# MLP rows stored once and scaled at the up-projection, memory rows normed behind the projection, weight sums and guards re-placed

## The chip, the cores and the metric

The kernel runs on one core of a Trainium2 chip. The metric is device microseconds (us) from the first to the last instruction of one launch. TensorE (PE) multiplies, VectorE (DVE), ScalarE (ACT) and GpSimd (POOL) work on rows in SBUF, SyncE (SP) issues nearly all transfers, in program order. Every engine takes its instructions strictly in the order in which the program stands.

## The reference

One hybrid decoder layer in fp32, 1024 tokens, width 1024:

```python
h = rms_norm(x, norm_mix_g)
# mLSTM, chunks of 128: needs C, n, m of the chunk before
y_m = sigmoid(mo) * rms_norm(mlstm_chunkwise(mq, mk, mv, ig, fg))
# causal differential attention, lam from lam_q1, lam_k1, lam_q2, lam_k2
y_d = diff_attention(dq, dk, dv, lam)
# attention into 256 memory rows
mkv = rms_norm(mem, mem_g) @ w_kv
y_c = memory_cross_attention(cq, mkv)
g_m, g_d, g_c = split(sigmoid(h @ w_gate + b_gate))
x = x + (g_m*(y_m @ w_proj_m) + g_d*(y_d @ w_proj_d) + g_c*(y_c @ w_proj_c)) @ w_out
h2 = rms_norm(x, norm_mlp_g)
x = x + square(relu(h2 @ w_up)) @ w_down      # width 4096
```

## The kernel before

**Products.** Each fp32 operand is cut into a high and a low part (`split`: ACT writes the rounded high part, L124, DVE subtracts it, L126; `split2` does the same at L117 and L69), and a product is three PE passes (`mm3`, L96). The large products use seven products of sums in place of eight (`PROD`): the sums of a weight's four quarters are four POOL additions (`wino_s`, L1292 to L1295, on tiles `wraw`), those of the activations are three DVE subtractions and one on POOL (`wino_t`, L1274 to L1277, from `xr` to `xts`); the cut results are `wo` and `xo`.

**Stages**, by the profile's clock: the memory rows' keys and values and the norm of x (0 to 67 us, `phase_x` and `mem_kv`); cross attention (to 180); mLSTM (to 560), in whose stream `early` forms weight sums ahead of time; differential attention (to 1115); gates (to 1208, `wino_gates`); the three projections (to 1434, `branches`, L1667); w_out (to 1523); up (to 1850, `wino`); down (to the end, `down`).

**Order.** A scheduler writes the instructions of each engine out in one order. `pin` fixes PE's. `issue_after` and `behind` set an instruction behind another on its engine (without a wait), `held` and `evicted` do so for a split against the last eviction of PSUM. `at(p, f)` in `early` hangs a step on position p of the mLSTM's PE stream.

**Start.** `consts` loads `vecs` (all vectors of gains, transposed to the tile `vec` at L221) and `lamv`, `gbias`; then the two tiles `mx` of memory rows are loaded and normed (`norm_rows`: Square on ACT L258, a POOL power, a DVE scaling L260), then transposed (L270) and cut to `memT`.

**mLSTM.** Chunks of 128 tokens carry a state `C`; `Ch` is its cut (COPY L771, then L773 for an update, L124 and L126). `mpT` is the cut matrix of decays, from the tile `ngb`, which SP loads (L721). `early` has `pairs` (4 loads, 4 sums L1452, 7 cuts L1490, 7 stores) and `sums` (4 loads, 4 sums L1452, 4 stores), all on tiles `es`.

**Gates.** `wino_gates` evicts PSUM with DVE additions to `u` and `c` (L1247 to L1261) while `wsp` cuts weights `w`.

**MLP.** In w_out, `res` makes x (tile `gl`, L1771), stores it (`x1_d`), squares it (L1779), adds it up on POOL (`ssq`, L1780), scales it by the MLP's gains (L1782, tile `h`) and stores that too (`h2_d`). `wino` loads `h2_d` to `xr` (`load`). The row norm comes late: `rstd` multiplies `ssq` with ones on PE (`px`, 8 small products), copies the result (`st`, L1833), and uses it on the products' results. `runs` is the order of products: run 0 takes two row blocks, run 1 four. The eight PSUM banks p0 to p7 are dealt in turn, `px` takes the eighth, which is also the first bank of the next run.

## Time and profile before

| | |
|---|---|
| runs | 2155.68, 2156.96, 2160.66 us (median 2156.96) |
| the profiled execution | 2153.97 us, span 2151.7 us |
| PE, DVE, ACT, POOL busy | 98%, 72%, 49%, 29% of the span |
| mean granted clock of PE | 0.996 |

PE is busy nearly throughout, so what is read in the profile is where PE stands still or runs at a lower clock. A row of the timeline gives start, length, engine, line, operation, output and inputs, shape and count, and in brackets the idle time ahead of it with what ended it.

### The profile page before, as it was taken

To read this page: it belongs to the slowest core of one execution; us is meant where nothing else is said; L and a number is where in the kernel's file an instruction comes from. 1 tells how busy PE (TensorE), PEld (TensorE's weight loads), DVE (VectorE), ACT (ScalarE), POOL (GpSimd) and SP (SyncE) were. 2 spreads that over 40 slices of the span, in tenths; PEclk is the share of its full clock that TensorE was granted. 3 is DMA by queue.
4 is the path that set the end of the run, shared out by engine and by line. 5 is a ranking of instruction groups with operands and counts; after the bars stand their busy time and mean duration, and the time that the engine had idled before them with its cause. 6 is when DMAs were issued, how large, how long until landed. Compare 5 with 4: busy or idle time off the path is not lost.

```text
span 2151.7 us, 31481 instructions
## 1 busy us (share of the span) xinstructions
PE 2112.8 (98%) x10905; PEld 1827.4 (85%) x10905; DVE 1559.6 (72%) x2971; ACT 1057.0 (49%) x2183; POOL 615.1 (29%) x756
## 2 busy tenths in 40 slices
...
GB/s 240 48 59 169 84 119 223 246 216 180 245 135 94 90 86 85 90 96 89 94 147 113 283 309 157 267 167 215 147 123 157 201 146 159 299 173 142 156 161 108
DMA packets 183206, 340.00 MB, mean 158 GB/s; under 512 B 17633, under 2 KB 52742, under 8 KB 180998
## 3 DMA queue, kind: packets, MB, share of 16 engines
...
q14 instruction: 74, 0.61, 0.1%
...
## 4 chain that ended last, share of the span: by engine, by line
PE 75%; DVE 8%; DMA 8%; ACT 3%; issue 2%; SPq 1%; POOL 1%; DVEq 0%; ACTq 0%; POOLq 0%
PE mm L96 27%; PE p L96 26%; PE mm L1667 11%; PE sc L96 5%; PE po L96 3%; PE tp L101 2%; DMA es<-in_wq 2%; DVE w L126 1%; DVE es L1452 1%; DVE cv L678 1%; DMA xr<-h_d 1%; SPq L1462 1%; PE pr L101 1%; DMA es<-y 1%; DMA wraw<-in_wdown 1%
## 5 line engine op out<-in xcount | busy, mean ns | idle before, releaser
L96 PE MATMUL mm<-w,hT 128*128 128x384 f32 (+3 forms) x2496 | 469.3, 331 | 1.3 <-DVE dsg L129 0.7
L96 PE MATMUL mm<-hT,w 128*128 128x512 f32 x1680 | 410.5, 395 | 0.3 <-ACT gt L503 0.3
L96 PEld LDWEIGHTS mm<-w,hT 128*128 128x128 f32 x2496 | 388.8, 189 | 11.9 <-DVE dsg L129 0.9
L96 PEld LDWEIGHTS mm<-hT,w 128*128 128x128 f32 x1680 | 309.9, 189 | 61.1 <-ACT gt L503 0.7
L96 PE MATMUL p<-xo,wo 128*128 128x512 f32 x1344 | 308.7, 392 | 0.0
L96 PE MATMUL p<-xd,wo 128*128 128x512 f32 x1344 | 305.6, 389 | 0.5 <-DVE acc L69 0.5
L96 PEld LDWEIGHTS p<-xo,wo 128*128 128x128 f32 x1344 | 253.6, 189 | 53.8 <-DVE u L69 1.0
L96 PEld LDWEIGHTS p<-xd,wo 128*128 128x128 f32 x1344 | 252.0, 188 | 53.9 <-DVE acc L69 1.4
L1667 PE MATMUL mm<-xs,w 128*128 128x512 f32 x1008 | 229.0, 389 | 1.0 <-DVE u L1261 1.0
L117 ACT CAST wo<-wraw 128x896 fp32r<-128x896 f32 x124 | 117.0, 945 | 226.3 <-POOL wraw L1295 94.6
L1667 PEld LDWEIGHTS mm<-xs,w 128*128 128x128 f32 x1008 | 189.1, 188 | 40.7 <-DVE u L1261 1.5
L69 DVE TENSOR_TENSOR wo<-wraw,wo 128x896 fp32r<-128x896 f32 x124 | 148.7, 1210 | 47.0 <-ACT wo L117 47.0
L1292 POOL TENSOR_TENSOR wraw<-wraw 128x128 f32<-128x128 f32 x128 | 101.1, 790 | 214.2 <-DMA wraw<-in_wdown 101.0
L1041 ACT ACTIVATE dpe<-sc,dst,drr 128x256 f32<-128x256 f32 (+7 forms) x128 | 106.7, 834 | 97.3 <-DVE dst L1037 96.1
L126 DVE TENSOR_TENSOR w<-raw,w 128x256 fp32r<-128x256 f32 (+4 forms) x257 | 127.6, 523 | 26.8 <-ACT w L124 26.1
L124 ACT CAST w<-raw 128x256 fp32r<-128x256 f32 (+4 forms) x257 | 114.9, 488 | 40.7 <-PE mm L96 11.6
L151 POOL TENSOR_SCALAR hss<-hss 128x4 f32<-128x4 f32 x8 | 3.9, 487 | 422.0 <-ACT mscr L785 422.0
L1033 DVE CUSTOM_DVE_ANT_0 sc<-sc,tmask 128x256 f32<-128x256 f32 (+7 forms) x128 | 97.1, 759 | 13.6 <-PE sc L96 12.8
L1294 POOL TENSOR_TENSOR wraw<-wraw 128x128 f32<-128x128 f32 x128 | 96.9, 757 | 0.0
L151 POOL TENSOR_SCALAR drr<-drr 128x16 f32<-128x16 f32 x16 | 3.3, 206 | 310.5 <-DVE drr L988 290.2
L96 PE MATMUL sc<-dk,dq 128*128 128x512 f32 (+3 forms) x384 | 91.9, 347 | 0.0
L69 DVE TENSOR_TENSOR acc<-acc,p 128x512 f32<-128x512 f32 x121 | 79.9, 684 | 14.5 <-PE p L96 13.9
...
## 6 DMA issues: line engine op xcount, KB each, us to landing
...
```

The costliest lines, as they stand in the source:

```text
L69: return self.tc.keep_in_program_order(f(*a, **k))
L96: ins = self.nc.tensor.matmul(out, l, r, start=start, stop=stop)
L101: self.pin(self.nc.tensor.transpose(out, x, self.ident))
L117: self.cast = self.A.copy(hi, src).ins
L124: a = nc.scalar.copy(hi, src)
L126: return a, nc.vector.tensor_sub(lo, src, f32(hi))
L678: V.scalar_tensor_tensor(out=c, in0=x[:, q : q + 512], scalar=cw(q), in1=c, op0=ALU.mult, op1=ALU.add)
L1033: V.tensor_tensor_reduce(out=sc[:, 0:n], in0=sc[:, 0:n], in1=self.tmask[:, D - n : D], scale=1.0, scalar=-3.0e38, op0=ALU.add, op1=ALU.max ...
L1041: nc.scalar.activation(pe[c][:, 0:n], sc[:, 0:n], AF.Exp, bias=t8[:, 2 + c : 3 + c], scale=rr[:, i, c : c + 1], accum_out=t8[:, 4 + c : 5 ...
L1292: G.tensor_add(r[:, 4], r[:, 0], r[:, 3])
L1294: G.tensor_sub(r[:, 6], r[:, 1], r[:, 0])
L1667: nc.tensor.matmul(cur[u], w[:, l, c], x[:, m], start=first and i == 0, stop=last and i == 2, skip_group_check=True)
```

## The change

**Start.** `consts` runs behind the issue of the memory loads; the part for lambda is now `lambdas`, behind the first half of x. The memory rows are not scaled ahead of the transposes; their factors (`rs`) are applied where the projection leaves PSUM.

**MLP.** The scaled copy of x (L1782) and its store are gone. `load` reads `x1_d` and scales it by the gains in SBUF, half on ACT, half on DVE. The guard that set the third activation block behind the last `res` now covers DVE, ACT and POOL, and stays until both products of run 0 are issued. `px` comes two tiles later. Banks are dealt from p0.

**Sums.** The positions of `early` move. In `wino_gates` the splits stand behind the last eviction. In `branches` the banks' halves change places.

```diff
-        lv = tmp.tile([P, 256], F32, name="lamv")
+    def lambdas(self, tmp):
...
     def norm_rows(self, src, r1, scr):
-        nc.scalar.activation(scr, src, AF.Square, accum_out=r1)
+        self.scale_rows(src, r1, scr)
+        self.nc.vector.tensor_scalar_mul(src, src, r1)
...
-            nc.scalar.copy(kr, ps)
+            nc.scalar.activation(kr, ps, AF.Copy, scale=rs[t])
-            nc.scalar.activation(scr[:, 0:512], ps, AF.Square)
+            nc.scalar.activation(scr[:, 0:512], ps, AF.Square, scale=rs[t])
-                self.split(self.mv[:, t, 0, s], self.mv[:, t, 1, s], ps)
+                self.split(self.mv[:, t, 0, s], self.mv[:, t, 1, s], ps, rs[t])
...
         mem = [load(a["mem"][t * P : (t + 1) * P, :], "mx") for t in range(2)]
-        for x in mem:
-            norm(x)
-        gen = self.mem_kv(kv, tmp, mem)
+        self.consts(tmp)
+        gen = self.mem_kv(kv, tmp, mem, [norm(x, "rm", self.scale_rows) for x in mem])
         half(0)
+        self.lambdas(tmp)
...
+                with self.held():
+                    self.split(t[:, 0], t[:, 1], raws[2 * u + kk][:, 1 + self.PROD[j][0]].rearrange("p k n -> p (k n)"))
...
-        with self.tc.issue_after(self.last_stt):
-            X[2] = self.wino_x(2, load)
+        guard = ExitStack()
+        for i in self.guard.values():
+            guard.enter_context(self.tc.issue_after(i))
+        X[2] = self.wino_x(2, load)
...
-            bank = lambda j: f"p{(7 * r + j + 4) % 8}"
+            bank = lambda j: f"p{(7 * r + j) % 8}"
-                    if (r, kp, j) in ((0, 1, 2), (1, 1, 3), (1, 2, 3), (1, 3, 3)):
+                    if (r, kp, j) in ((0, 1, 4), (1, 1, 3), (1, 2, 3), (1, 3, 3)):
                         first(bank(7))
+                if n == 1:
+                    guard.close()
...
-            at(p - (16 if p > 124 else 8), load)
+            at(p - {110: 40, 124: 8}.get(p, 14), load)
-                at(p + 4 + i, lambda i=i: keep(i))
+                at(p + 3 + i, lambda i=i: keep(i))
-        for n, p in enumerate((106, 124, 202, 266, 330, 394, 458, 522)):
+        for n, p in enumerate((110, 124, 198, 262, 326, 390, 454, 518)):
-                sums(p + 10, 8, 11, *S.pop(0))
-                sums(p + (22 if n < 7 else 18), 7, 9, *S.pop(0))
+                sums(p + 8, 7, 9, *S.pop(0))
+                sums(p + 18, 7, 10, *S.pop(0))
...
-                        self.pmm.tile([P, 512], F32, tag=f"mm{g % 2 * 4 + (u + 2) % 4}", name=self.name("mm")) for u in range(4)
+                        self.pmm.tile([P, 512], F32, tag=f"mm{4 - g % 2 * 4 + u}", name=self.name("mm")) for u in range(4)
-                    self.nmm = 3
+                    self.nmm = 7
...
-                            h = op.tile([P, 512], F32, tag="h2", name=self.name("h2"))
-                            nc.scalar.activation(h, x, AF.Copy, scale=self.vec[:, R_MLP + f : R_MLP + f + 1])
-                            nc.sync.dma_start(half(self.h2d, f, hf), h)
...
-                        self.h2d[2 * kp : 2 * kp + 2].rearrange("k p n -> p k n"),
+                        self.x1d[2 * kp : 2 * kp + 2].rearrange("k p n -> p k n"),
+                    f = R_MLP + 2 * kp
+                    nc.scalar.activation(b[:, 0:2], b[:, 0:2], AF.Copy, scale=self.vec[:, f : f + 1])
+                    nc.vector.tensor_scalar_mul(b[:, 2:4], b[:, 2:4], self.vec[:, f + 1 : f + 2])
```

Three places show how the instructions move. The first is the mLSTM's first chunk on SP: `es` loads of the first pair (L1482, after L1497) against the loads of `wib` and `ngb`. Before:

```order
L695 DMA wib_347_2465<-g_dwi 128x4x128
L1482 DMA es_340_2426<-in_wq 128x256
L588 DMA g_dec_2371<-g_dd 128x32
L1482 DMA es_341_2427<-in_wq 128x256
L1482 DMA es_342_2428<-in_wq 128x256
L1482 DMA es_343_2429<-in_wq 128x256
L721 DMA ngb_349_2471<-g_dng 128x4x128
L695 DMA wib_415_2890<-g_dwi 128x4x128
L504 DMA gates<-gt_344_2452 128x512
L721 DMA ngb_422_2926<-g_dng 128x4x128
```

After, where the `es` loads stand ahead of the gate stores:

```order
L1497 DMA es_312_2236<-in_wq 128x256
L1497 DMA es_313_2237<-in_wq 128x256
L1497 DMA es_314_2238<-in_wq 128x256
L1497 DMA es_315_2239<-in_wq 128x256
L593 DMA g_dwi<-g_u_2190 32x128
L592 DMA g_dng<-g_c_2195 32x128
L594 DMA g_dd<-g_mp_2356 32x1
L703 DMA wib_347_2455<-g_dwi 128x4x128
L729 DMA ngb_349_2461<-g_dng 128x4x128
L596 DMA g_dec_2369<-g_dd 128x32
```

The `es` loads have left the place between the gate stores and the `ngb` load.

The same place on DVE, where `ks` and `mpT` are what the chunk's products read. Before:

```order
L725 TENSOR_TENSOR ngb_349_2471<-ngb_349_2471,tmaskT_101 128x512
L1452 TENSOR_TENSOR es_352_2495<-es_341_2427,es_340_2426 128x256
L129 SCALAR_TENSOR_TENSOR ks_351_2483<-tp_350_2478,g_col_2459,ks_351_2483 128x128
L1452 TENSOR_TENSOR es_340_2426<-es_340_2426,es_343_2429 128x256
L1452 TENSOR_TENSOR es_353_2496<-es_340_2426,es_341_2427 128x256
L129 SCALAR_TENSOR_TENSOR ks_351_2483<-tp_350_2478,g_col_2459,ks_351_2483 128x128
L1452 TENSOR_TENSOR es_354_2497<-es_342_2428,es_353_2496 128x256
L129 SCALAR_TENSOR_TENSOR ks_351_2483<-tp_350_2478,g_col_2459,ks_351_2483 128x128 x2
L744 TENSOR_TENSOR ngb_349_2471<-ngb_349_2471,tp_355_2502 128x512
L1490 TENSOR_TENSOR es_340_2426<-es_340_2426 128x256
L126 TENSOR_TENSOR mpT_356_2516<-ngb_349_2471,mpT_356_2516 128x512
```

After:

```order
L733 TENSOR_TENSOR ngb_349_2461<-ngb_349_2461,tmaskT_58 128x512
L129 SCALAR_TENSOR_TENSOR qp_348_2458<-wib_347_2455,qp_348_2458 128x512
L606 COPY g_col_2449<-tp_345_2445 128x96
L129 SCALAR_TENSOR_TENSOR ks_351_2473<-tp_350_2468,g_col_2449,ks_351_2473 128x128 x4
L752 TENSOR_TENSOR ngb_349_2461<-ngb_349_2461,tp_352_2485 128x512
L126 TENSOR_TENSOR mpT_353_2499<-ngb_349_2461,mpT_353_2499 128x512
L1467 TENSOR_TENSOR es_354_2514<-es_313_2237,es_312_2236 128x256
L1467 TENSOR_TENSOR es_312_2236<-es_312_2236,es_315_2239 128x256
```

The sums now stand behind the cut of `mpT`.

The second place is the start of the MLP on DVE: `gl` is the last w_out tile, `xts` and `xo` the third block's sums and cuts, `wo` cut weights, `st2` the copy of `px`, `dg` its use. Before:

```order
L1771 SCALAR_TENSOR_TENSOR gl_2857_16499<-mm_2856_16474,gl_2857_16499 128x512
L1274 TENSOR_TENSOR xts_2872_16679<-xr_2871_16677 128x512
L126 TENSOR_TENSOR xo_2873_16684<-xr_2871_16677,xo_2873_16684 128x3x512
L1276 TENSOR_TENSOR xts_2872_16679<-xr_2871_16677,xts_2872_16679 128x512
L1277 TENSOR_TENSOR xts_2872_16679<-xr_2871_16677,xts_2872_16679 128x512
L1833 COPY st2_16759<-px_2886_16750 128x8
L69 TENSOR_TENSOR wo_2887_16788<-wraw_2876_16698,wo_2887_16788 128x7x128
L126 TENSOR_TENSOR xo_2873_16684<-xts_2872_16679,xo_2873_16684 128x4x512
L1838 TENSOR_SCALAR dg_16858<-ident_68,st2_16759 128x128
```

After:

```order
L1786 SCALAR_TENSOR_TENSOR gl_2842_16444<-mm_2841_16419,gl_2842_16444 128x512
L1823 TENSOR_SCALAR xr_2855_16623<-xr_2855_16623,vec_119 128x1024
L1285 TENSOR_TENSOR xts_2856_16627<-xr_2855_16623 128x512
L1287 TENSOR_TENSOR xts_2856_16627<-xr_2855_16623,xts_2856_16627 128x512
L126 TENSOR_TENSOR wo_2859_16643<-wraw_2851_16603,wo_2859_16643 128x7x128
L1288 TENSOR_TENSOR xts_2856_16627<-xr_2855_16623,xts_2856_16627 128x512
L126 TENSOR_TENSOR xo_2857_16632<-xr_2855_16623,xo_2857_16632 128x3x512
L69 TENSOR_TENSOR wo_2868_16680<-wraw_2858_16637,wo_2868_16680 128x7x128
L126 TENSOR_TENSOR xo_2857_16632<-xts_2856_16627,xo_2857_16632 128x4x512
L1848 COPY st2_16713<-px_2870_16704 128x8
L69 TENSOR_TENSOR wo_2871_16736<-wraw_2860_16646,wo_2871_16736 128x7x128
L1853 TENSOR_SCALAR dg_16808<-ident_105,st2_16713 128x128 x3
```

The copy `st2` stood ahead of the 128x4x512 cut of the third block and now stands behind it.

The same place on POOL: `ssq` is the sum of squares, `wraw` are weights, `xts` is the third block. Before:

```order
L1275 TENSOR_TENSOR xts_2872_16679<-xr_2871_16677 128x512
L1780 TENSOR_TENSOR ssq_13576<-ssq_13576,sq_2850_16433 128x512
L1780 TENSOR_TENSOR ssq_13576<-ssq_13576,sq_2854_16468 128x512
L1292 TENSOR_TENSOR wraw_2888_16791<-wraw_2888_16791 128x128
L1294 TENSOR_TENSOR wraw_2888_16791<-wraw_2888_16791 128x128
L1293 TENSOR_TENSOR wraw_2888_16791<-wraw_2888_16791 128x128
L1295 TENSOR_TENSOR wraw_2888_16791<-wraw_2888_16791 128x128
L1780 TENSOR_TENSOR ssq_13576<-ssq_13576,sq_2858_16503 128x512
L1292 TENSOR_TENSOR wraw_2876_16698<-wraw_2876_16698 128x128
L1294 TENSOR_TENSOR wraw_2876_16698<-wraw_2876_16698 128x128
L1293 TENSOR_TENSOR wraw_2876_16698<-wraw_2876_16698 128x128
L1295 TENSOR_TENSOR wraw_2876_16698<-wraw_2876_16698 128x128
```

After:

```order
L1795 TENSOR_TENSOR ssq_13566<-ssq_13566,sq_2843_16448 128x512
L1303 TENSOR_TENSOR wraw_2858_16637<-wraw_2858_16637 128x128
L1305 TENSOR_TENSOR wraw_2858_16637<-wraw_2858_16637 128x128
L1304 TENSOR_TENSOR wraw_2858_16637<-wraw_2858_16637 128x128
L1306 TENSOR_TENSOR wraw_2858_16637<-wraw_2858_16637 128x128
L1303 TENSOR_TENSOR wraw_2860_16646<-wraw_2860_16646 128x128
L1286 TENSOR_TENSOR xts_2856_16627<-xr_2855_16623 128x512
L1304 TENSOR_TENSOR wraw_2860_16646<-wraw_2860_16646 128x128
L1305 TENSOR_TENSOR wraw_2860_16646<-wraw_2860_16646 128x128
L1306 TENSOR_TENSOR wraw_2860_16646<-wraw_2860_16646 128x128
```

The last sum of squares now stands ahead of the weight sums and of the third block's `xts`, which stood far ahead of it.

The same place on ACT, from the last square of w_out on; `pt` (L1382) and `u2` are evictions of PSUM, L117 and L124 the casts of weights and blocks. Before:

```order
L1779 ACTIVATE sq_2858_16503<-gl_2857_16499 128x512
L1782 ACTIVATE h2_2859_16506<-gl_2857_16499,vec_79 128x512
L117 CAST wo_2887_16788<-wraw_2876_16698 128x7x128
L124 CAST xo_2873_16684<-xts_2872_16679 128x4x512
L1382 COPY pt0_16775<-p0_2877_16704 128x512
L1382 COPY pt1_16776<-p1_2878_16705 128x512
```

After:

```order
L1794 ACTIVATE sq_2843_16448<-gl_2842_16444 128x512
L1822 ACTIVATE xr_2855_16623<-xr_2855_16623,vec_119 128x1024
L124 CAST wo_2859_16643<-wraw_2851_16603 128x7x128
L124 CAST xo_2857_16632<-xr_2855_16623 128x3x512
L117 CAST wo_2868_16680<-wraw_2858_16637 128x7x128
L117 CAST wo_2871_16736<-wraw_2860_16646 128x7x128
L124 CAST xo_2857_16632<-xts_2856_16627 128x4x512
L1397 COPY pt0_16723<-p0_2861_16652 128x512
```

Between the last square and the cast of the block's last four sums stood one weight cast and the old scaling; now the new scaling, the block's first cast and three weight casts stand there.

The third place is a later chunk of the mLSTM on DVE, at the first copy of the state `C`; `es` are the 512-wide sums of `sums`. Before:

```order
L1452 TENSOR_TENSOR es_504_3399<-es_504_3399,es_503_3398 128x512
L725 TENSOR_TENSOR ngb_589_3910<-ngb_589_3910,tmaskT_101 128x512
L771 COPY C_521_3506<-sc_520_3499 128x258
L126 TENSOR_TENSOR Ch_522_3508<-C_521_3506,Ch_522_3508 128x258
L781 TENSOR_TENSOR den_523_3511<-den_523_3511,g_col_2459 128x1
L782 RECIPROCAL den_523_3511<-den_523_3511 128x1
L1452 TENSOR_TENSOR es_525_3530<-es_514_3480,es_513_3479 128x512
L773 SCALAR_TENSOR_TENSOR C_527_3545<-C_521_3506,g_dec_2371,sc_526_3535 128x258
L1452 TENSOR_TENSOR es_513_3479<-es_513_3479,es_516_3482 128x512
L126 TENSOR_TENSOR Ch_528_3547<-C_527_3545,Ch_528_3547 128x258
```

After:

```order
L1467 TENSOR_TENSOR es_501_3353<-es_501_3353,es_500_3352 128x512
L1467 TENSOR_TENSOR es_516_3472<-es_510_3426,es_509_3425 128x512
L779 COPY C_522_3505<-sc_521_3498 128x258
L1467 TENSOR_TENSOR es_509_3425<-es_509_3425,es_512_3428 128x512
L126 TENSOR_TENSOR Ch_523_3507<-C_522_3505,Ch_523_3507 128x258
L1467 TENSOR_TENSOR es_510_3426<-es_509_3425,es_510_3426 128x512
```

The second group of `es` sums moves from behind the first `Ch` to both sides of the copy `C`.

59 lines of the change are left out of this document (30 added, 29 removed).

## The prediction

> **What bounds the kernel now.** I read the busy times first, then the chain of work that ended last, then what PE waited for, then the stretches and single instructions around those waits.
>
> ```profile
> PE 2112.8 (98%) x10905; PEld 1827.4 (85%) x10905; DVE 1559.6 (72%) x2971; ACT 1057.0 (49%) x2183; POOL 615.1 (29%) x756
> PE 75%; DVE 8%; DMA 8%; ACT 3%; issue 2%; SPq 1%; POOL 1%; DVEq 0%; ACTq 0%; POOLq 0%
> ```
>
> PE is busy for 98% of the span and carries 75% of the chain (the next, DVE and DMA, 8% each). The change leaves the products themselves alone, so it can only win time in which PE stands still or runs below full clock. The first is a list of waits.
>
> ```profile
> PE tp L270 <- DVE mx L260: 5.0, 2, 4.9
> PE px L96 <- POOL ssq L1780: 4.9, 1, 4.9
> PE sc L96 <- ACT mpT L124: 3.1, 1, 3.1
> PE sc L96 <- DVE Ch L126: 2.2, 4, 1.2
> PE mm L96 <- DVE u L1252: 1.5, 1, 1.5
> PE sc L96 <- ACT Ch L124: 1.4, 3, 0.7
> PE mm L1667 <- DVE u L1261: 1.0, 1, 1.0
> PE mm L96 <- DVE c L1247: 0.6, 2, 0.4
> ```
>
> The columns are total us, times, longest. Nearly every wait that the edits aim at stands here once, with its price. The second is the clock, the column after POOL's in the table of stretches:
>
> ```profile
> 256.00:268.00 12.00, 8.91 (x33) 7.13 (x32) 7.59 (x21) 6.28 (x19) 0.00 (x0) 0.72 0.51 177
> 1523.00:1546.00 23.00, 17.82 (x72) 14.60 (x71) 11.09 (x10) 13.09 (x17) 17.80 (x22) 0.78 0.53 176
> 1546.00:1850.00 304.00, 303.98 (x1348) 251.20 (x1347) 255.57 (x304) 144.41 (x210) 197.19 (x261) 1.00 0.48 166
> ```
>
> Two waits, of 3.1 and 4.9 us, are followed by a granted clock of 0.72 and 0.78 in their stretch, so they cost more than they last. In the up-projection behind them PE is busy 303.98 of 304 us: 1348 products in that time are 0.226 us each, the price of a wide product below.
>
> **The change part by part.** All sums are against the profiled execution's 2153.97 us (2.27 us of it outside the span of 2151.7). It lies 2.99 us under the median of 2156.96, which I add at the end.
>
> *Start: 2.2 us saved, ends 0 and 4.9.*
>
> ```profile
> 0.72 0.39 SPq L242 DMA_DIRECT2D lamv<-in_lamv  x1
> 2.08 1.36 SPq L320 DMA_DIRECT2D mx<-in_mem  x2
> 7.88 1.06 ACT L258 ACTIVATE scr<-mx 128x1024 f32<-128x1024 f32 x1 [3.19 <-DMA mx<-in_mem]
> 10.40 1.04 ACT L124 CAST w<-raw 128x1024 fp32r<-128x1024 f32 x1
> 13.12 2.36 DVE L126 TENSOR_TENSOR w<-raw,w 128x1024 fp32r<-128x1024 f32 x2
> 12.05 0.69 PE L270 MATMUL tp<-ident,mx 128*128 128x128 f32 x2 [4.87 <-DVE mx L260]
> 14.38 1.22 PE L96 MATMUL mm<-w,memT 128*128 128x512 f32 x2
> ```
>
> The memory loads are issued at 0.72 in place of 2.08, and the Square and the first weight's cast follow the load: 10.40 becomes 9.04, ending at 10.1. The scalings that hold PE until 12.05 go, and PE's 4.87 us wait with them. But DVE's order now has the first weight's subtraction (1.2 us, half of 2.36) ahead of the copy to `vec`, which every cut of `memT` needs: subtraction to 11.3, copy and cut to 12.2, where 0.9 is an estimate below the 1.6 us between the end of the first transposes (12.74) and the first product, in which the cut lay. The first product then starts at 12.2 instead of 14.38. The row factors are applied in instructions that run anyway. Lambda's six small instructions go behind the first half of x, where the splits ahead of them are what PE has in store; if that cover is gone they cost a wait as long as they are, small against the 4.9. If the weight loads decide, nothing is won; if `vec` did not matter, PE's whole 4.87.
>
> *First chunk of the mLSTM: 5.9 us saved, ends 2 and 6.5.*
>
> ```profile
> 247.16 2.61 SPq L1482 DMA_DIRECT2D es<-in_wq  x3
> 249.87 0.38 SPq L721 DMA_DIRECT2D ngb<-g_dng  x1
> 254.50 0.69 DVE L725 TENSOR_TENSOR ngb<-ngb,tmaskT 128x512 f32<-128x512 f32 x1 [5.33 <-DMA ngb<-g_dng]
> 260.07 1.31 PE L96 MATMUL sc<-va,mpT 128*128 128x258 f32 x3 [3.09 <-ACT mpT L124]
> 261.18 5.32 PE L96 MATMUL mm<-hT,w 128*128 128x512 f32 x12
> 266.30 0.61 PE L96 MATMUL sc<-va,ks 128*128 128x258 f32 x3
> ```
>
> The `ngb` load waited behind three `es` issues for 2.6 us, its consumer stood idle until 254.50, and then four `es` sums and a cut stood between it and `mpT`. Afterwards neither is there: the load comes 2.6 us earlier and five DVE instructions are out of the way, against a wait of 3.09. The wait goes, and with it the slow clock behind it: 12 products took 5.32 where 12 x 0.226 are 2.71, 2.6 lost, and the three `sc` took 1.31 against 0.61, 0.7 lost. 3.09 + 2.6 + 0.7 = 6.4 (the upper end, rounded up). What is late next is the first `Ch`, as in other chunks (rows above, longest 1.2); I leave 0.5 for it. The lower end is a wait that stays at 1 with most of the clock loss.
>
> *Other sums of the mLSTM: 1.5 us saved, ends -4 and 3.6.*
>
> ```profile
> 517.64 0.69 DVE L1452 TENSOR_TENSOR es<-es,es 128x512 f32<-128x512 f32 x1 [4.09 <-DMA es<-y]
> 519.23 0.39 PE L96 MATMUL sc<-Ch,qp 128*128 128x258 f32 x1 [0.68 <-ACT Ch L124]
> 520.78 0.50 PE L96 MATMUL sc<-Ch,qp 128*128 128x258 f32 x2 [1.17 <-DVE Ch L126]
> ```
>
> DVE waits up to 4.09 us for an `es` load, and the update of `C` that PE needs stands behind that. Of that PE waited 0.68 + 1.17 = 1.85. The sum of all `Ch` waits in the list is 3.6 us. The second group of sums is moved to both sides of the first copy of `C`, away from the later updates, but the load's lead stays at 7 positions for the second group and falls from 8 to 7 for the first (a position is three products, 0.68 us). So a wait can as well come back at the first copy. I take two fifths of the waits, since more leaves the updates than comes to the copy; the lower end is six first groups later by 0.68 us, 4.1, of which most reaches PE.
>
> *Gates: 1.8 us saved, ends 0 and 2.1.*
>
> ```profile
> 1115.00:1208.00 93.00, 90.01 (x393) 72.61 (x391) 57.57 (x101) 46.47 (x97) 25.56 (x32) 1.00 0.48 156
> 1137.15 4.15 DVE L126 TENSOR_TENSOR w<-fr,w 128x256 fp32r<-128x256 f32 x5 [1.44 <-ACT w L124]
> ```
>
> Five splits ran ahead of the eviction that PE waited for at L1252. With `held` a split issued behind an eviction stays behind it; the sum of the two waits is 2.1, of which one small `c` wait may stay. The cover for the splits is DVE's idle time (57.57 of 93 us busy); if it is gone, weights come late and nothing is won.
>
> *Banks in the projections: 1.0 us saved, ends 0 and 1.0.* The first projection tiles no longer take the banks that the gates' last evictions hold, so the L1261 wait of 1.0 goes. Elsewhere the rotation is the same.
>
> *Start of the MLP: 2.1 us saved, ends -1.3 and 6.9.*
>
> ```profile
> 1531.51 1.14 POOL L1292 TENSOR_TENSOR wraw<-wraw 128x128 f32<-128x128 f32 x1 [3.99 <-DMA wraw<-in_wup]
> 1534.46 0.46 POOL L1295 TENSOR_TENSOR wraw<-wraw 128x128 f32<-128x128 f32 x1
> 1534.87 1.26 POOL L1780 TENSOR_TENSOR ssq<-ssq,sq 128x512 f32<-128x512 f32 x1
> 1523.73 1.29 POOL L1275 TENSOR_TENSOR xts<-xr 128x512 f32<-128x512 f32 x1 [7.96 <-DMA xr<-h_d]
> 1536.18 1.87 PE L96 MATMUL px<-ones,ssq 128*128 128x1 f32 x8 [4.94 <-POOL ssq L1780]
> 1537.91 6.31 PE L96 MATMUL p<-xo,wo 128*128 128x512 f32 x16
> 1537.93 0.94 ACT L117 CAST wo<-wraw 128x896 fp32r<-128x896 f32 x1 [6.52 <-POOL wraw L1295]
> 1538.78 1.89 ACT L124 CAST xo<-xts 128x2048 fp32r<-128x2048 f32 x1
> 1540.71 2.29 DVE L126 TENSOR_TENSOR xo<-xts,xo 128x2048 fp32r<-128x2048 f32 x1 [0.61 <-ACT xo L124]
> ```
>
> Before, the stretch lost 23 - 17.82 = 5.2 us idle, 16 products took 6.31 against 3.62 (2.7), and `px`, by the same ratio, 0.8 of its 1.87: 8.7. The 16 scalings and 16 stores go, and ACT no longer waits for a free `h` buffer ahead of the casts and squares. The up-products begin at 1523.0; eviction and square of the last tile I estimate at 0.8 us each from instructions of that width (0.69 at 254.50), `ssq` with its 1.26 ends at 1525.9. `px` is two tiles later, at 1523.0 + 36 x 0.226 = 1531.2, so it waits for nothing, and PE comes to the next run's first tile 1.8 us of `px` and 6 products later, at 1534.35. That tile has `px`'s bank, so it needs the copy `st2`, and this stands on DVE behind the third block's last cut. Queued in that chain, by the rows: POOL's four weight sums, which took from 1531.51 to 1534.92, to 1529.4; one of the next four at 0.46 and `xts` at 1.29 to 1531.1; the other three at 0.46 to 1532.5; ACT's weight cast 0.94 and block cast 1.89 to 1535.3; DVE's cut 2.29 to 1537.6. PE waits 3.3 us, a little longer than the 3.09 that brought half clock, and pays 3.3 for that as at the first chunk: 6.6 against 8.7. With all of POOL's additions at 0.46 the copy comes at 1536.1, a wait of 1.8 with the clock kept: 6.9 saved. With both sets slow it comes at 1539.2, and with 0.61 more at each of three hand-overs, as at 1540.71, at 1541: 6.7 + 3.3 = 10.0, a loss of 1.3. I take one slow set and one fast because the rows have both and DVE is full with the block's scaling and cuts only at first. The new scaling (1.06 on ACT, like the Square of that size at 7.88; DVE's half no row gives, at most 1.2 as a subtraction of that size) lies within this chain for the third block; for the first two it lies under w_out's products, and if that cover is gone the up-projection starts later by as much.
>
> The trace has 3.09 us of idle time followed by half clock. The Trainium skill, "TensorE: Matmul & The Clock Gate", Part 1, section "The HAM clock gate", says that the clock falls after at least one idle window of about 3.4 us, and that the windows run free of the kernel. By that rule a new wait of 3.3 us would leave the clock alone, and the sum would be 3.3 larger; the 3.09 us row speaks against it, and the sum here goes by the row.
>
> Sum: 2.2 + 5.9 + 1.5 + 1.8 + 1.0 + 2.1 = 14.5, so 2139.5 us against the profiled execution, and with 2.99 for the median 2142.5.
>
> **The rivals.**
> 1. *The copy comes early enough.* POOL's short additions, a wait of 1.8 and no slow clock: 4.8 more saved, 2137.7. For it: the row of 0.46; against it: the row of 1.14, while DVE works.
> 2. *The copy's wait leaves the clock alone.* Then only 3.3 is paid: 3.3 more saved, 2139.2. For it: the forecast wait is hardly longer than the shortest that brought half clock; against it: both long waits in this trace did bring it. The Trainium skill's rule (page and section as above) is this rival's reason beside the rows.
> 3. *One new wait at a first copy of `C`.* A stop of 3.09 with its slow clock costs 6.4, and the 1.5 is not won: 2150.4. For it: DVE waited 4.09 on a load; against it: only 1.85 us of that reached PE.
> 4. *Slower than before.* Load leads of 7 positions (4.8 us) are too short for the first groups: the 4.09 us wait reached PE for 1.85, so 2.24 are covered, and a wait of DVE of 2.24 + 3.09 = 5.3 us stops PE long enough for half clock. At three of the twelve groups that is 19.2, with the 1.5: 2163.2; from three on it decides.
> 5. *The start and the banks don't do what they say:* the weight loads, not the norm, set the first product, and another eviction holds the projections: 2142.5 + 2.2 + 1.0 = 2145.7.
>
> **How the numbers follow.** The forecast has 0.40, rivals 1 to 5 have 0.20, 0.10, 0.17, 0.06 and 0.07. The range 2130 to 2154 holds all but rival 4 and the tails of 1 and 3: below 2137.7 it reaches by the other upper ends (start 2.7, sums 2.1, and most of the rest), above 2150.4 by the lower end of the first chunk (3.9). A measurement of this kernel tells about 0.2% (4.3 us) from no change: faster means under 2152.6. The forecast, 1, 2 and 5 are faster, and of rival 3, whose centre lies 2.2 below that, some six tenths: faster 0.87, same 0.07, slower 0.06.
>
> **What would show it.** The first product starts near 12.2 us. No wait of a `sc` for `mpT`, and a clock of 1.00 from 256 to 268. No L1252 and L1261 waits on PE. `px` without a wait, and in its place a wait of a `p` tile for the `st` copy, of 2 to 6 us, with a clock under 0.9 behind it. Wrong would be: a clock below 1.00 anywhere in the mLSTM, a `memT` wait as long as before, or a `p` that waits for weights in the up-projection.

## The result, and the profile after

| | before | after |
|---|---|---|
| median of the runs | 2156.96 us | 2145.61 us |
| lowest, highest (5 runs each) | 2155.68, 2162.48 | 2142.31, 2150.22 |
| the profiled execution | 2153.97, span 2151.7 | 2145.61, span 2143.8 |

The ratio of the times is 0.9944 [0.9923, 0.9964]: 11.35 us less by the medians, 8.36 by the two profiled executions. The forecast was 2142.5 in 2130 to 2154. The page's busy times and chain, and the list of waits of PE, of the changed kernel:

```profile
PE 2110.5 (98%) x10905; PEld 1827.3 (85%) x10905; DVE 1561.0 (73%) x2973; ACT 1050.6 (49%) x2171; POOL 618.9 (29%) x756
PE 82%; DVE 7%; DMA 5%; ACT 3%; issue 2%; POOL 1%; SPq 1%; DVEq 0%; ACTq 0%; POOLq 0%
PE p L96 <- ACT pt L1397: 6.0, 1, 6.0
PE sc L96 <- ACT Ch L124: 4.1, 2, 3.4
PE tp L277 <- DVE vec L224: 2.4, 1, 2.4
PE mm L96 <- DVE va L126: 1.3, 3, 0.6
```

PE now carries 82% of the chain instead of 75%. Four of the waits shown of before are gone from the list: `px` for `ssq` (4.9), `sc` for `mpT` (3.1), `mm` for `u` at the gates (1.5) and at the projections (1.0). The one for `mx` (5.0) is halved, now for `vec`; but PE's wait for the load of the vectors ahead of it, in neither extract, grew from 6.7 to 8.0. Two are new or much longer: a product tile `p` of the up-projection waits 6.0 us, a `sc` waits 3.4 for `Ch`. `va` grew from 0.3 to 1.3. The stretches around the first chunk, the last chunks and the start of the MLP (columns as in the prediction; the clock stands after POOL):

```profile
252.00:268.00 16.00, 16.00 (x88) 13.83 (x86) 11.29 (x33) 8.78 (x27) 0.00 (x0) 1.00 0.60 197
520.00:560.00 40.00, 36.18 (x211) 31.63 (x209) 25.20 (x64) 17.62 (x49) 2.08 (x2) 0.96 0.58 186
1515.00:1546.00 31.00, 24.98 (x111) 20.51 (x110) 20.93 (x25) 15.58 (x19) 23.82 (x29) 0.89 0.27 86
```

The first chunk runs at full clock without a gap (16.00 of 16 us busy); the last chunks and the MLP's start do not (0.96 and 0.89).

A view of one operand gives the first and the last start of the products that read it. The same products run in both kernels, so their starts split the span. Before, then after:

```profile
L96 PE MATMUL sc<-mkT,cqT x96: 277/283/387, 74.3 to 139.9; 128*128 128x256 f32 x96
L96 PE MATMUL sc<-va,mpT x96: 278/283/583, 260.1 to 565.0; 128*128 128x258 f32 x96
L1667 PE MATMUL mm<-xs,w x1008: 387/389/504, 1205.9 to 1435.5; 128*128 128x512 f32 x168
L96 PE MATMUL sc<-mkT,cqT x96: 277/283/385, 73.1 to 138.5; 128*128 128x256 f32 x96
L96 PE MATMUL sc<-va,mpT x96: 278/282/288, 255.5 to 562.8; 128*128 128x258 f32 x96
L1682 PE MATMUL mm<-xs,w x1008: 389/389/389, 1200.7 to 1429.0; 128*128 128x512 f32 x168
```

Worked out in this way for every kernel of this study: A up to the first `mkT` product, B from there to the first `mpT`, C from the first to the last `mpT` (the mLSTM's chunks), D to the first `xs` (differential attention and gates), E over the `xs` products (projections), F from the last `xs` to the end of the span (w_out and the MLP).

| us | A | B | C | D | E | F |
|---|---|---|---|---|---|---|
| before | 74.3 | 185.8 | 304.9 | 640.9 | 229.6 | 716.2 |
| after | 73.1 | 182.4 | 307.3 | 637.9 | 228.3 | 714.8 |
| e1 copy first | 72.5 | 182.5 | 306.2 | 637.6 | 228.3 | 715.5 |
| e2 evictions first | 72.2 | 182.8 | 308.5 | 637.5 | 228.2 | 714.9 |
| e3 old sums | 73.4 | 184.8 | 305.3 | 638.3 | 228.2 | 715.9 |
| e4 first pair only | 72.3 | 182.5 | 302.7 | 637.7 | 228.2 | 715.3 |
| e5 stores later | 73.1 | 182.5 | 299.9 | 639.4 | 228.3 | 716.8 |
| e6 gates undone | 72.9 | 182.4 | 307.3 | 642.3 | 229.5 | 714.9 |
| e7 vec first | 73.5 | 183.3 | 303.7 | 640.5 | 228.2 | 716.0 |
| e8 evictions, first pair | 73.4 | 182.5 | 304.5 | 639.1 | 228.2 | 715.7 |
| e9 start undone | 74.3 | 182.3 | 303.3 | 640.3 | 228.3 | 717.0 |
| e10 MLP undone | 73.3 | 182.3 | 305.4 | 639.6 | 228.2 | 711.3 |
| e11 all remedies | 72.4 | 182.0 | 303.9 | 637.9 | 228.2 | 710.4 |

Each is one execution. Kernels that share a stage's code show what that is worth: E agrees within 0.1 us, C of the changed table of sums (after, e1, e2, e6, e7, e9, e10) runs from 303.3 to 308.5, D of the changed gates from 637.5 to 640.5, F of the changed MLP (after, e3 to e7, e9, where F isn't touched) from 714.8 to 717.0. A difference of 2 or 3 us in C, D or F from one trace alone says little.

By the table, the 7.9 us between the two spans are 1.2 in A, 3.4 in B, -2.4 in C, 3.0 in D, 1.3 in E and 1.4 in F. C before held the slow clock behind the `mpT` wait (3.3 by the prediction's rows); that gain is in C too, so the rest of C lost 5.7 in this pair of traces.

**The last chunk**, where most of that is. Timeline of SP, DVE and PE of the changed kernel (`y` is the loaded operand of `sums`, `xc_d` their store):

```profile
543.47 2.25 SPq L1485 DMA_DIRECT2D xc_d<-es  x3
545.82 0.95 SPq L1477 DMA_DIRECT2D es<-y  x2
550.04 0.69 DVE L1467 TENSOR_TENSOR es<-es,es 128x512 f32<-128x512 f32 x1 [4.66 <-DMA es<-y]
552.52 0.48 DVE L781 SCALAR_TENSOR_TENSOR C<-C,g_dec,sc 128x258 f32<-128x258 f32 x1
553.49 1.01 PE L96 MATMUL sc<-Ch,qp 128*128 128x258 f32 x3 [3.40 <-ACT Ch L124]
554.34 4.51 PE L96 MATMUL mm<-hT,w 128*128 128x512 f32 x12
```

The last two loads stand on SP behind three stores of the group before (2.25 us, from 543.47 on; the last of the four sums to be stored runs on DVE only at 544.69). DVE idles 4.66 us on them, and behind the sums stands the update of `C` (L781), for whose cut PE waits 3.40 us. Behind it 12 products take 4.51 where 2.71 is full clock (1.8 lost). The `sc` take 1.01 against 0.52 in the chunk before, which is no slow clock: in e5 and e9 below they take 0.97 and 1.00 at the same place with the clock at 1.00. Together 3.40 + 1.8 + 0.5 = 5.7.

**The start of the MLP.** Timelines of PE, DVE, ACT and POOL of the changed kernel:

```profile
1516.55 8.32 PE L96 MATMUL p<-xo,wo 128*128 128x512 f32 x36
1524.71 1.84 PE L96 MATMUL px<-ones,ssq 128*128 128x1 f32 x16
1534.08 14.14 PE L96 MATMUL p<-xo,wo 128*128 128x512 f32 x54 [6.02 <-ACT pt L1397]
1531.61 2.29 DVE L126 TENSOR_TENSOR xo<-xts,xo 128x2048 fp32r<-128x2048 f32 x1 [5.26 <-ACT xo L124]
1533.82 0.16 DVE L1848 COPY st<-px 128x8 f32<-128x8 f32 x1
1529.61 1.89 ACT L124 CAST xo<-xts 128x2048 fp32r<-128x2048 f32 x1
1531.41 3.50 ACT L1397 COPY pt<-p 128x512 f32<-128x512 f32 x7
1518.30 1.30 POOL L1795 TENSOR_TENSOR ssq<-ssq,sq 128x512 f32<-128x512 f32 x1 [4.15 <-ACT sq L1794]
1522.68 0.79 POOL L1306 TENSOR_TENSOR wraw<-wraw 128x128 f32<-128x128 f32 x1
1523.43 1.97 POOL L1303 TENSOR_TENSOR wraw<-wraw 128x128 f32<-128x128 f32 x1
1525.36 2.13 POOL L1286 TENSOR_TENSOR xts<-xr 128x512 f32<-128x512 f32 x1
1527.45 0.46 POOL L1304 TENSOR_TENSOR wraw<-wraw 128x128 f32<-128x128 f32 x1
1531.82 2.39 POOL L1306 TENSOR_TENSOR wraw<-wraw 128x128 f32<-128x128 f32 x1
```

`px` runs without a wait. Six products later PE stops for 6.02 us, and 54 products then take 14.14 us where 54 x 0.226 are 12.2: 1.9 of slow clock, 7.9 together. The bracket names the eviction `pt`, whose seven copies ran from 1531.41 on; the copy `st` at 1533.82 to 1533.98 ends just ahead of PE's start. Which of the two PE needed is what the first experiment asks.

### The profile page after: what moved, and what is told of

Read it like the earlier page. It is cut to its first block, busy times and chain, and to the rows that moved or that the text cites. A ratio compares the mean times of both kernels' runs of the same rounds, so it can differ in the third digit from the quotient of the medians.

```text
span 2143.8 us, 31457 instructions
## 1 busy us (share of the span) xinstructions
PE 2110.5 (98%) x10905; PEld 1827.3 (85%) x10905; DVE 1561.0 (73%) x2973; ACT 1050.6 (49%) x2171; POOL 618.9 (29%) x756
## 3 DMA queue, kind: packets, MB, share of 16 engines
HBM read 214.15 MB, written 94.40 MB: 144 GB/s over the span
## 4 chain that ended last, share of the span: by engine, by line
PE 82%; DVE 7%; DMA 5%; ACT 3%; issue 2%; POOL 1%; SPq 1%; DVEq 0%; ACTq 0%; POOLq 0%
PE mm L96 34%; PE p L96 26%; PE mm L1682 11%; PE sc L96 5%; PE po L96 3%; PE tp L101 2%; DMA es<-in_wq 1%; DVE w L126 1%; DMA raw<-in_wkv 1%; DVE cv L686 1%; DMA es<-y 1%; DVE es L1467 1%; DMA ngb<-g_dng 1%; PE pr L101 1%; DVE acc L69 1%
## 5 line engine op out<-in xcount | busy, mean ns | idle before, releaser
L117 ACT CAST wo<-wraw 128x896 fp32r<-128x896 f32 x124 | 116.9, 945 | 226.7 <-PE p L96 92.7
L1303 POOL TENSOR_TENSOR wraw<-wraw 128x128 f32<-128x128 f32 x128 | 100.8, 788 | 205.6 <-DMA wraw<-in_wdown 99.9
L124 ACT CAST w<-raw 128x256 fp32r<-128x256 f32 (+4 forms) x257 | 116.4, 488 | 45.1 <-PE mm L96 11.8
L1041 DVE CUSTOM_DVE_ANT_0 sc<-sc,tmask 128x256 f32<-128x256 f32 (+7 forms) x128 | 97.1, 758 | 13.1 <-PE sc L96 12.2
L1305 POOL TENSOR_TENSOR wraw<-wraw 128x128 f32<-128x128 f32 x128 | 94.6, 739 | 0.0
L1306 POOL TENSOR_TENSOR wraw<-wraw 128x128 f32<-128x128 f32 x128 | 88.8, 694 | 10.0
```

The source lines that it names most:

```text
L117: self.cast = self.A.copy(hi, src).ins
L124: a = nc.scalar.copy(hi, src)
L1041: V.tensor_tensor_reduce(out=sc[:, 0:n], in0=sc[:, 0:n], in1=self.tmask[:, D - n : D], scale=1.0, scalar=-3.0e38, op0=ALU.add, op1=ALU.max ...
L1303: G.tensor_add(r[:, 4], r[:, 0], r[:, 3])
L1305: G.tensor_sub(r[:, 6], r[:, 1], r[:, 0])
L1306: G.tensor_sub(r[:, 7], r[:, 2], r[:, 5])
```

## The experiments

Ratios are against the kernel before on the same chip.

**e1: the copy ahead of the third block's last cut.** The split of `xts` is set behind the copy `st`.

```diff
-        self.split(xo[:, 3:7, 0], xo[:, 3:7, 1], t)
+        late.append(lambda: self.split(xo[:, 3:7, 0], xo[:, 3:7, 1], t))
...
+                    if (r, kp, j) == (0, 1, 4):
+                        with self.tc.issue_after(self.stc):
+                            rest[0]()
```

> The changed kernel with one instruction order altered: on VectorE the copy of the row norm's product (st) stands ahead of the third block's last cut; ScalarE's order stays. Theory: the 6.0 us wait of PE at the start of the up-projection, which the list of waits puts down to ScalarE's evictions pt, ends with the copy st, since its next product starts at 1534.08 and the copy ends at 1533.98. Then PE takes its first tile of the second run at once and waits one tile later for the first pt, which ends at 1531.9: a wait of about 3 us, and 2 us less in all. Rival (the list is right, pt ends it): the wait stays at 6.0 and the first tile of the second run starts at 1534.

One run: 2144.41 us (before on this chip 2155.54). Timeline of DVE and PE:

```profile
1524.49 0.17 DVE L1855 COPY st<-px 128x8 f32<-128x8 f32 x1 [0.23 <-PE px L96]
1529.98 14.58 PE L96 MATMUL p<-xo,wo 128*128 128x512 f32 x51 [3.32 <-ACT pt L1404]
```

The copy came right behind `px`, at 1524.49 instead of 1533.82, and PE's wait fell from 6.02 to 3.32: the copy was what PE waited for, and the evictions are next in line. But 51 products then took 14.58 us against 11.5 at full clock: 3.1 of slow clock where 1.9 stood behind the longer wait. Wait and clock together are 6.4 against 7.9, and F is 715.5 against 714.8: nothing that a trace can tell.

**e2: the evictions ahead too.** As e1, and ACT's cast stands behind the first run's evictions. The edit also sets the fourth block and the `dg` scalings behind the third block's last cut on DVE.

```diff
-                    A.copy(t, m)
-                wsp(n)
+                    c = A.copy(t, m)
+                with self.tc.issue_after(self.stc), self.tc.issue_after(c.ins):
+                    self.cut = rest[0]()[1].ins
+                    wsp(n)
```

> The changed kernel with the third block's last cut (ScalarE and VectorE) and the fifth weight's set behind both the copy st and the seven evictions pt. Theory: the wait of 6.0 us and the 1.7 us of slower products behind it go, none takes their place, so 7 to 8 us less than the changed kernel: near 2138, ratio to before 0.991. Rival (the block's cut, started later, is late for the fifth product group): the wait only moves 9 us on, less than 3 us saved, near 2144.

2144.35 us (2140.10 to 2145.92), ratio 0.994 [0.9927, 0.9953]. Timeline of PE:

```profile
1526.62 13.91 PE L96 MATMUL p<-xo,wo 128*128 128x512 f32 x60
1543.97 0.91 PE L96 MATMUL px<-dg,ones 128*128 128x128 f32 x4 [3.00 <-DVE dg L1861]
```

The stop is gone: 60 products run through in 13.91 us. The next is 17 us on: the `dg` tiles made from `st`, which the edit set back on DVE, stop PE for 3.00. The wait has moved, as the rival said (near 2144), and F stays at 714.9.

**e3: the old table of sums in the changed kernel.**

```diff
-            at(p - {110: 40, 124: 8}.get(p, 14), load)
+            at(p - (16 if p > 124 else 8), load)
...
-        for n, p in enumerate((110, 124, 198, 262, 326, 390, 454, 518)):
+        for n, p in enumerate((106, 124, 202, 266, 330, 394, 458, 522)):
...
-                sums(p + 8, 7, 9, *S.pop(0))
-                sums(p + 18, 7, 10, *S.pop(0))
+                sums(p + 10, 8, 11, *S.pop(0))
+                sums(p + (22 if n < 7 else 18), 7, 9, *S.pop(0))
```

> The changed kernel with the old table of positions for the weight sums in the mLSTM; all else as changed. Theory: the table wins 6.5 at the first chunk and gives back 5.5 in the later chunks, above all with one wait of 3.4 us and slow clock at the last chunk: so within 2 us of the changed kernel, 2145 to 2148, with the first chunk's 3.1 us wait for mpT back and no wait over 1.5 us in the later chunks. Rival (the last chunk's wait is chance of one execution): 6 us slower than the changed kernel, 2152.

2148.29 us (2146.05 to 2152.30), ratio 0.9967 [0.9957, 0.9977]. The list of waits of PE:

```profile
PE sc L96 <- ACT mpT L124: 2.3, 1, 2.3
```

The `mpT` wait is back (B is 2.4 longer), the one of 3.4 in the last chunk is not there. The whole table is worth about 2 us by the trace (span 2145.9 against 2143.8), 2.7 by the medians and some 5 by the ratios, whose intervals overlap (0.9957 to 0.9977 and 0.9923 to 0.9964). By the traces it is small because the table wins at the first chunk and loses at the last.

**e4: the new place for the first pair only**, the old table for the rest:

```diff
-            at(p - {110: 40, 124: 8}.get(p, 14), load)
+            at(p - {110: 40, 124: 8}.get(p, 16), load)
...
-        for n, p in enumerate((110, 124, 198, 262, 326, 390, 454, 518)):
+        for n, p in enumerate((110, 124, 202, 266, 330, 394, 458, 522)):
```

(and `sums` as in e3.)

> The changed kernel with the old table but for the first pair of sums, which stands at position 110 and loads 40 positions ahead as in the change. Theory: the first chunk's wait stays away and the later chunks are as before, so about 5.5 us less than the changed kernel: near 2140, ratio 0.992. Rival (the later chunks' waits come with the new first pair or are chance): no difference from the changed kernel, 2145.

2143.61 us (2140.53 to 2145.72), ratio 0.9938 [0.9925, 0.9951]. B is as short as in the changed kernel (182.5) and C 302.7, less than in any kernel with the changed table; e8 and e11, which have the same table, show 304.5 and 303.9. By the means the later groups' new positions cost some 2 us of C (306.0 over the seven with the changed table, 303.7 over these three), but single kernels of the two groups overlap, and the timed ratio shows what the rival said, no difference (0.9938 against 0.9944).

**e5: one number of the table.** The stores of the first group of `sums` in each round go three positions later, from p + 17 to p + 20, and so behind the second group's loads at p + 18.

```diff
-                sums(p + 8, 7, 9, *S.pop(0))
+                sums(p + 8, 7, 12, *S.pop(0))
```

> The changed kernel with one number altered: in the mLSTM the stores of each first group of weight sums stand 3 positions later, so that on SP the loads of the second group go ahead of them. Theory: the 3.4 us wait for Ch at the last chunk comes from these stores, which wait on SP for late sums and hold back the second group's loads (es<-y, 4.7 us late on VectorE). With the loads first, VectorE no longer waits over 2 us there, PE's wait falls under 1 us, and with the slow clock behind it some 4 to 5 us go: near 2141. Rival (the loads are late because the first group's own loads are): the wait stays over 2.5 us and the time at 2145.

2142.81 us (2141.67 to 2146.50), ratio 0.9947 [0.9933, 0.9961]. Timeline of DVE and PE in the last chunk:

```profile
542.87 2.15 DVE L1467 TENSOR_TENSOR es<-es,es 128x512 f32<-128x512 f32 x3 [1.85 <-DMA es<-y]
547.85 0.97 PE L96 MATMUL sc<-Ch,qp 128*128 128x258 f32 x3 [2.24 <-ACT Ch L124]
548.66 2.91 PE L96 MATMUL mm<-hT,w 128*128 128x512 f32 x12
```

DVE's wait falls from 4.66 to 1.85, PE's from 3.40 to 2.24, and no slow clock follows (12 products in 2.91 against 4.51). C is 299.9, 3.4 below the shortest with the changed table.

The six other kernels with that table (e1, e2, e6, e7, e9, e10) have the same order on SP. There DVE waits 3.86 to 4.49 us at this place and PE 2.29 to 2.90, with half clock behind it in four and none in e7 (2.50) and e9 (2.29); in the kernels with the old later table (before, e3, e4, e8, e11) PE doesn't stop here; there it waits a chunk earlier, 0.68 to 1.55 and then 1.17 or 1.18 us. So the stores ahead of the loads are shown as the cause of DVE's wait. Of PE's stop they are a part only: the theory wanted it under 1 us, and 2.24 are left, since DVE works without a break from 542.87 to the update of `C` at 546.88, on four sums and four weights' cuts that stand ahead of it. In the timed runs e5 can't be told from the changed kernel.

**e6: gates and banks undone.**

```diff
-                with self.held():
-                    self.split(t[:, 0], t[:, 1], raws[...])
+                self.split(t[:, 0], t[:, 1], raws[...])
...
-    tag=f"mm{4 - g % 2 * 4 + u}"
+    tag=f"mm{g % 2 * 4 + (u + 2) % 4}"
...
-                    self.nmm = 7
+                    self.nmm = 3
```

> The changed kernel without the hold on the gates' weight splits and with the old banks in the projections; all else as changed. Theory: the waits for u at L1252 (1.5 us, now another line number) and L1247, and the 1.0 us wait of the first projection tile come back: 3 to 4 us more than the changed kernel, near 2149, and the gates and the head of the projections show 4.2 us more lost time. Rival (these waits were chance of the order that the scheduler writes, not of hold and banks): less than 1 us of them comes back, 2146.

2150.92 us (2148.23 to 2153.92), ratio 0.9983 [0.9974, 0.9992]. The list of waits of PE:

```profile
PE mm L96 <- DVE c L1236: 1.5, 1, 1.5
PE mm L96 <- DVE u L1236: 1.5, 1, 1.5
```

The gates' waits are back, D is 642.3 and E 229.5. This is the only part whose undoing the timed runs show: the intervals of the ratios do not touch (0.9964 and 0.9974), and their middles are 0.39% (8 us) apart, the medians themselves 5.3. By the traces it is 3.6 in D (against the mean, 638.7, of the kernels with the changed gates) and 1.3 in E, 4.9 together, where the prediction put it at 2.8. What makes the rest of the 8 us no trace shows. Hold and banks were undone together; by its place, the 1.3 in E is the banks'.

**e7: the copy to `vec` ahead of the first weight's cut.**

```diff
+        with self.tc.issue_after(self.vc):
+            w = self.load_w(a["wkv"][0], 512, 2)
```

> The changed kernel with the copy to vec ahead of the first weight's subtraction on VectorE. Theory: the first product of the memory projection starts 1 to 2 us earlier (12.46 becomes 10.5 to 11.5), but the transposes of the first keys (28.5) stay within 0.4 us, since the later weights' loads set them: the start's gain is limited by these loads, not by vec. Rival (vec is what eats the forecast gain): the keys' transposes come 1 us or more earlier, and the whole start with them.

One run: 2147.04 us (before on this chip 2154.73). Timelines of PE, changed kernel first, then e7:

```profile
12.46 3.83 PE L96 MATMUL mm<-w,memT 128*128 128x512 f32 x10
28.50 0.43 PE L310 MATMUL tp<-ident,kr 128*128 128x128 f32 x2 [1.24 <-DVE kr L307]
12.25 4.28 PE L96 MATMUL mm<-w,memT 128*128 128x512 f32 x10 [2.10 <-ACT memT L128]
25.74 0.63 PE L311 MATMUL tp<-ident,kr 128*128 128x128 f32 x3 [1.21 <-DVE kr L308]
```

The first product gains 0.2 only, since `memT` is then late: on ACT its cut stands behind the second weight's cast. The keys' transposes come 2.8 us earlier, and at the first `mkT` product nothing of it is left (A is 73.5 against 73.1). Neither theory had this. What takes the lead back between the two was not followed.

**e8: e2 and e4 together,** with one more guard on POOL and the eight `dg` scalings moved from DVE to ACT.

```diff
+                if n == 1:
+                    with self.tc.issue_after(self.pw_):
+                        raw()
...
-                    wsp(n)
+                    wsp(n, more=n > 0)
```

(`pw_` is POOL's power of the row norm, so that it runs ahead of the next weight sums.)

> Both remedies together: the old table of sums but for the first pair, and at the start of the up-projection the copy st and the evictions ahead of the third block's last cut, with the eight scalings dg on ScalarE and the row norm's power ahead of one more set of weight sums on POOL. Theory: the mLSTM as in the run with the first pair only (5 us less lost than in the changed kernel), the 6.0 us wait gone, and the 3.0 us wait for dg that took its place in the run with the evictions first gone too: 10 to 12 us less than the changed kernel, 2133 to 2136, ratio 0.990. Rival (VectorE and POOL are full in the first 25 us of the up-projection, so some wait of 2 to 3 us comes back at the third or fourth block): 5 to 7 us less, 2139 to 2141.

2141.33 us (2139.99 to 2145.20), ratio 0.9936 [0.9922, 0.9949]. The `dg` stop is gone, and the next comes (timeline of PE):

```profile
1546.43 4.63 PE L96 MATMUL p<-xo,wo 128*128 128x512 f32 x10 [3.12 <-DVE wo L69]
```

3.12 us for a weight's cut, 10 products then in 4.63 instead of 2.26. The wait has moved a second time, and the time is near the rival's (2139 to 2141), not the theory's.

**e9: the start undone** (`consts` ahead of the memory rows, the rows scaled ahead of the transposes).

```diff
-            nc.scalar.activation(kr, ps, AF.Copy, scale=rs[t])
+            nc.scalar.copy(kr, ps)
...
-        gen = self.mem_kv(kv, tmp, mem, [norm(x, "rm", self.scale_rows) for x in mem])
+        for x in mem:
+            norm(x)
+        gen = self.mem_kv(kv, tmp, mem)
```

> The changed kernel with the start as before (vectors, lambda and gate bias loaded first, memory rows normed ahead of their transposes); all else as changed. Theory: the 1.9 us that the first product gained are mostly given back by 73 us, where the changed kernel was 1.2 us ahead, so about 1.2 us more than the changed kernel: 2146 to 2147, which a measurement can hardly tell from no difference. Rival (the start is worth what its first wait was, 4.9 us): 2150.

2146.61 us (2142.72 to 2147.35), ratio 0.9966 [0.9954, 0.9977]. A is 74.3 as before, against 72.2 to 73.5 in the others (mean 72.9): by that mean the start is worth 1.4 us, too little for the timed runs, whose intervals overlap.

The others fall into two groups. In e1, e2, e4 and e11 A is 72.2 to 72.5; in the changed kernel, e3, e5, e6, e8 and e10 it is 72.9 to 73.4. The stretch from 34 to 42 us tells them apart, here in e4 and in the changed kernel:

```profile
34.00:42.00 8.00, 6.18 (x31) 4.45 (x32) 5.92 (x14) 5.87 (x12) 4.70 (x9) 1.00 0.40 159
34.00:42.00 8.00, 6.77 (x28) 5.33 (x29) 5.23 (x13) 5.32 (x10) 4.75 (x9) 0.79 0.45 180
```

The granted clock is 1.00 in the first group and 0.79 in the second. So the start is worth 1.8 to 2.1 us where the clock stays up and 0.9 to 1.4 where it falls; the kernel before and e9 kept it up (1.00). Only e7, with its other order, has 73.5 at full clock.

**e10: the MLP undone**: the scaled copy stored, the old guard, `px` and banks, in the changed kernel.

```diff
+                            h = op.tile([P, 512], F32, tag="h2", name=self.name("h2"))
+                            nc.scalar.activation(h, x, AF.Copy, scale=self.vec[:, R_MLP + f : R_MLP + f + 1])
+                            nc.sync.dma_start(half(self.h2d, f, hf), h)
...
-            bank = lambda j: f"p{(7 * r + j) % 8}"
+            bank = lambda j: f"p{(7 * r + j + 4) % 8}"
...
-                    if (r, kp, j) in ((0, 1, 4), (1, 1, 3), (1, 2, 3), (1, 3, 3)):
+                    if (r, kp, j) in ((0, 1, 2), (1, 1, 3), (1, 2, 3), (1, 3, 3)):
```

> The changed kernel with w_out and the start of the up-projection as before (scaled copy of x stored and loaded, guard on VectorE alone, px two tiles earlier, old banks); all else as changed. Theory: the old 4.9 us wait of px with its slow clock comes back and the 6.0 us wait for the copy st goes, so the loss there is 8 to 9 us in place of 8: within 1.5 us of the changed kernel, 2145 to 2147. Rival (the 16 stores less also make the stages around it faster, or the slow clock costs more before): 4 us or more above the changed kernel.

2142.54 us (2139.62 to 2147.70), ratio 0.9956 [0.9943, 0.9968]. Neither theory held: the wait of 4.9 at `px` does not come back, and F is 711.3, the shortest but one. A row of PE in e10, ACT's last scaling but one in the kernel before and in e10, what followed it before on DVE and SP, and the transfers of the scaled copy around that place (size, median us to landing), before and e10:

```profile
1525.37 1.05 PE L96 MATMUL px<-ones,ssq 128*128 128x1 f32 x8 [0.24 <-POOL ssq L1791]
1524.99 0.72 ACT L1782 ACTIVATE h<-gl,vec 128x512 f32<-128x512 f32 x1 [5.74 <-DMA h_d<-h]
1514.18 0.72 ACT L1793 ACTIVATE h<-gl,vec 128x512 f32<-128x512 f32 x1 [1.74 <-DMA h_d<-h]
1526.58 1.89 DVE L126 TENSOR_TENSOR wo<-wraw,wo 128x896 fp32r<-128x896 f32 x1 [8.06 <-ACT wo L124]
1528.50 1.36 SPq L1306 DMA_DIRECT2D wraw<-in_wup  x3
h_d<-h SPq DMA_DIRECT2D x5, 256.0 KB, 7.4
h_d<-h SPq DMA_DIRECT2D x6, 256.0 KB, 3.8
```

The order on POOL around `ssq` is the same in both programs. In the kernel before, ACT's scaling waited 5.74 us for a buffer whose store was slow (7.4 us, median of five); behind it on ACT stood a weight's cast, behind that on DVE its cut (to 1528.47), behind that on SP the next weights' loads (1528.50), and behind these on POOL the four weight sums from 1531.51 on, with `ssq` last (1534.87, in the prediction's rows). The last square was not what `ssq` waited for: it ended at 1530.80. In e10 the stores landed in 3.8, ACT waited 1.74, and `px` 0.24. By these rows the 8.7 us that the prediction read at this place were largely the price of a late store, not of the old order alone. Why the stores land sooner in e10 was not tried, and one trace each does not tell whether they do so in every execution.

**e11: all remedies**: e2 and e4, the `dg` tiles made on ACT, and the fourth block's and a weight's cuts set behind the work that PE waits for.

```diff
-                        for t in range(NT):
-                            V.tensor_scalar_mul(dg[:, t], self.ident, st[:, t : t + 1])
+                    with self.tc.issue_after(self.xsc):
+                        for t in range(NT):
+                            nc.scalar.activation(dg[:, t], self.ident, AF.Copy, scale=st[:, t : t + 1])
```

> As the run with evictions and first pair, but with the row norm's power ahead of only the seventh weight's sums, the fourth block's POOL sum ahead of the eighth weight's sums, and the sixth weight's cut on VectorE ahead of the fourth block's cuts. Theory: the 3.1 us wait for wo that was left there came from the sixth weight standing behind the fourth block on VectorE; with it ahead, no wait over 1 us is left in the first 30 us of the up-projection: 2135 to 2138, ratio 0.990 to 0.991. Rival (the fourth block is then late, since POOL and VectorE are full): a wait of 2 to 3 us for xo, 2140 to 2142, no better than that run.

2137.77 us (2136.17 to 2141.41), ratio 0.9932 [0.9918, 0.9945]. Timeline of PE and stretch of the MLP's start:

```profile
1541.30 1.43 PE L96 MATMUL p<-xo,wo 128*128 128x512 f32 x5 [1.23 <-DVE xo L126]
1510.00:1545.00 35.00, 33.77 (x165) 28.21 (x164) 22.57 (x20) 21.84 (x31) 30.91 (x32) 1.00 0.29 92
```

The longest stop left there is 1.23 us, at full clock (1.00), and F is 710.4. The time is inside the theory's 2135 to 2138, the ratio above its 0.990 to 0.991. It has the lowest median of all, 0.7% under the kernel before. Its interval overlaps that of the changed kernel, so that it beats that one is likely by the traces and not shown by the times.

## Why the prediction was right, and where it was not

The sum against the profiled execution was 14.5 us. What the pair of traces shows is 7.9 in the span. The medians lie 11.35 apart, because the execution profiled before was 2.99 under its median and the one after is the median itself. So the median came within 3.1 us of its forecast partly by luck: against the sum's own 2139.5 the profiled execution is 6.1 us too long.

| step | forecast | measured in the two traces |
|---|---|---|
| start | 2.2 | 1.2 (A; 1.8 to 2.1 where the clock stays up, by e9) |
| first chunk | 5.9 | 6.7 (B, and the clock in C) |
| other sums | 1.5 | -5.7 (the rest of C) |
| gates | 1.8 | 3.0 (D; 3.6 by e6) |
| banks | 1.0 | 1.3 (E) |
| start of the MLP | 2.1 | 1.4 (F) |

- *Start: right, and of the right size where the clock stays up.* The first product came at 12.46 (forecast 12.2, before 14.38), with the first weight's subtraction, the copy to `vec` and the cut of `memT` in the order derived. One time in it is right by luck: the first weight's cast came at 9.13 (forecast 9.04), but the Squares had come 3.4 us earlier (4.44 for 7.88), and ACT then waited 2.30 us for the weight's load. Of the first product's 1.9 us, 1.2 are left at the first `mkT` product; in e1, e2, e4 and e11, with the same start, it is 1.8 to 2.1. What the changed kernel lacks against those comes with the low clock near 36 us (e9's rows), which the step didn't have. Why some executions have it was not tried.
- *First chunk: right.* No wait for `mpT`, clock 1.00.
- *Other sums: the step that failed, in size and sign.* It took the sum of the `Ch` waits as what could go and bounded the loss at 4 by the loads' shorter leads. What came is one long stop (3.40 + 1.8 + 0.5 = 5.7), rival 3's mechanism at 5.7 instead of 6.4, at an update of `C` in the last chunk rather than at a first copy. The prediction's own sign of being wrong came with it: a clock below 1.00 in the mLSTM (0.96 from 520 to 560). The lead in positions was the wrong quantity; what counts is what stands ahead on SP. In `sums(p, q, r, ...)` the loads hang at p, the sums at p + q, the stores at p + r. In the old table the last round's second loads were at p + 18 and the first group's stores at p + 21 (`22 if n < 7 else 18`, the exception for the last round); the new one has the stores at p + 17, ahead of the loads. That stood in the diff, and the step did not read it. e5 shows by moving only the stores that they hold back the loads and DVE; of PE's stop 2.24 us stay, for the sums and cuts that stand on DVE ahead of the update. 5.7 is also one execution's figure: in e7 and e9, with the same table, the stop is 2.50 and 2.29 with no slow clock, and by the means of C (e4) the later positions cost some 2 us. The sign of the step is wrong by all the traces' means, its size is open, and the timed runs don't show it.
- *Gates and banks: right, too small.* The waits at the gates and at the projections are gone. The forecast priced the waits shown, 2.1 and 1.0; e6 shows more, 3.6 and 1.3 by the traces. Of the 3.6, 3.0 are the two waits of its list; why `c` waits 1.5 there and 0.6 before was not looked into.
- *Start of the MLP: the mechanism right, two sizes off, which nearly cancel.* The wait for the copy `st` came where it was forecast (e1), with 6.02 us for 3.3 and 1.9 of slow clock for 3.3: 7.9 for 6.6. From the first product the chain stood at 3.05 us for `ssq` (forecast 2.9), 6.9 after the first four weight sums (6.4), 10.9 after `xts` (8.1) and 17.4 after the copy (14.6). The term that failed is the second set of POOL's additions: one addition and `xts` took 1.97 + 2.13 = 4.10 us instead of 0.46 + 1.29, since DVE was still busy. The lower end of the step had both sets slow.
- *The price of before* was taken from one trace as the price of the old order. By e10 a late store made most of it. With the old MLP in the changed kernel F is 3.5 us shorter in one trace (711.3 against 714.8), and the timed ratios overlap (0.9956 and 0.9944). So no run shows that the MLP's part of the change won anything.

Of the rivals, 1 and 2 did not come, 4 neither (one such stop, not three), 5 in part (the start gave 1.2 of 2.2; the banks did what they say).

Removing 16 stores brought no gain of its own that shows: the bytes written to HBM fell from 98.60 to 94.40 MB, and the one wait that went with them in these rows is ACT's for its buffer.
